# Attention scores from five products of one height: rotary parts of queries and keys stacked to 128 rows per head

## The chip, the cores and the metric

The kernel runs on one core of a Trainium2 chip. The metric is the device time of one execution in microseconds. Engine names in the profile: PE is TensorE (PEld its weight loads), DVE is VectorE, ACT is ScalarE, POOL is GpSimd, SP is SyncE, which issues nearly all DMAs.

## What is computed

Two blocks in a row on 512 tokens of width 1024, all in float32: first a convolution and state-space layer, then two transformer-like layers with feed-forward halves before and after a mixer. The mixer of the second of these layers is latent attention with eight heads; it is the part that matters here:

```python
MLA_HEADS, NOPE_DIM, ROPE_DIM, V_DIM = 8, 128, 64, 128      # QK_DIM = 192
q = (_rmsnorm(c_q, q_a_norm) @ w_q_up).reshape(B, T, 8, 192)
kv = (_rmsnorm(c_kv, kv_a_norm) @ w_kv_up).reshape(B, T, 8, 256)
k = concat([kv[..., :128], broadcast(k_pe)], -1)
q, k = _rmsnorm(q, q_norm), _rmsnorm(k, k_norm)
q = concat([q[..., :128], _rope(q[..., 128:], cos, sin)], -1)
k = concat([k[..., :128], _rope(k[..., 128:], cos, sin)], -1)
s = einsum('bhqd,bkhd->bhqk', q, k) * 192 ** -0.5           # causal mask, softmax
o = einsum('bhqk,bkhd->bqhd', softmax(s), v)
```

A score is a sum over 192 elements per head: 128 without position and 64 rotary ones. The rotary key is the same for all heads but for its norm.

## The kernel before

Activations lie with channels on the 128 partitions and the 512 tokens along the row. Every float32 product is made of three products of a reduced type: each operand is split into a high part (a cast on ACT) and a low part (the rest, a subtraction on DVE), and high x high, high x low and low x high are summed in one bank of PSUM. Weights are streamed by `wload` (L226 to L239): SP loads a tile `raw`, ACT casts it to `wh`, DVE (sometimes POOL) subtracts to `wl`. `mm3` (L241 to L250) issues the three products of L247 to L249.

The program is a row of stages: the first block, a feed-forward half, the mixer `even`, two feed-forward halves, the mixer `odd` (about 2050 to 2350 us on the profile's clock), a last feed-forward half. A list scheduler with priorities sets the order of the instructions on each engine when the kernel is built, so a change anywhere can move instructions elsewhere in the program.

In `odd`, after the projections, heads are worked in four pairs p. `kpair(p)` prepares the keys of a pair: rows of norms are read from a DRAM scratch `nd` and repeated over the partitions (L1781 for the 128-element part, L1785 in two halves of 64 partitions for the rotary part), multiplied by the keys (L1787, on POOL for the tiles in `KP_POOL`, else DVE) and split (L253 and L254) into three tiles high and low: the 128-row part of each of the two heads, and one tile whose lower 64 rows are the rotary key of the first head and whose upper 64 rows that of the second. `qpair(p)` makes the queries in the same layout, two tiles of 128 rows and one shared rotary tile, split at L254 by `P.split(ro, hi, lo)`. `head(h, K, Q)` then works four blocks of 128 queries. Per block b it sums six score products at L1872 over N = 256, 256, 384 and 512 keys, in turns one of 128 rows and one of 64 rows, adds the mask by a product at L1873, and goes on: row maximum (L1875, DVE), scaled negative (L1877, DVE), exponential with sum (L1879, ACT), reciprocal and scaling (L1880 and L1881, DVE), transposes (L1884, PE), split (L1887 on ACT, L1888 on DVE). After four blocks the products with the values follow (L1895 to L1897), all 128 rows high. Two PSUM banks take the scores in turn and two the transposes.

While the heads of pair p run, `kpair(p + 1)` and `qpair(p + 1)` stand between them, in p = 0 also half of the value projection (`vproj(1)`), and from p = 2 on half of the output projection (`outp(0)`), whose products come at L247 to L249 with the name `s`. `TSlots` hands out `OD_S` tiles of 512 columns in turn.

Of the kernel before, what the change touches and what calls it, by code (L numbers as in the profile page):

```python
# [8 lines left out]
F32 = mybir.dt.float32  # L9
# [4 lines left out]
T = 512  # L14
# [142 lines left out]
class Prog:  # L157
    def __init__(self, ctx, tc, ap):
        self.tc, self.nc, self.ap = tc, tc.nc, ap
        nc = self.nc  # L160
        E = ctx.enter_context
        self.const = E(tc.tile_pool(name="const", bufs=1))
        self.res = E(tc.tile_pool(name="res", bufs=1))
        self.wr = E(tc.tile_pool(name="wr", bufs=2))
        self.whp = E(tc.tile_pool(name="whp", bufs=2))
        self.wlp = E(tc.tile_pool(name="wlp", bufs=2))
        psum = E(tc.tile_pool(name="psum", bufs=1, space=PSUM))
        self.banks = [psum.tile([128, T], F32, name=f"bank{i}") for i in range(8)]
        self.rot = {}
        self.use_banks(mm=4, sd=4)  # L170
        self.vec = self.const.tile([128, NVEC], F32, name="vec")
        nc.gpsimd.dma_start(self.vec, ap["vec"])
        self.ones = self.const.tile([128, 128], F32, name="ones")
        nc.vector.memset(self.ones, 1.0)
        self.ident = self.const.tile([128, 128], F32, name="ident")
        nc.gpsimd.affine_select(out=self.ident, in_=self.ones, pattern=[[1, 128]], base=0,
                                channel_multiplier=-1, compare_op=ALU.is_equal, fill=0.0)
        self.eps6 = self.const.tile([128, 1], F32, name="eps6")
        nc.vector.memset(self.eps6, 1e-6)
        self.eps5 = self.const.tile([128, 1], F32, name="eps5")  # L180
        nc.vector.memset(self.eps5, 1e-5)
        self.xa = self.res.tile([128, 8 * T], F32, name="xa")
        self.x = self.cut(self.xa)
        self.new_xhl()
        self.rs = None
        self.ph = None
        self.wlo = nc.vector
# [840 lines left out]
def even(P, nxt):  # L1028
# [8 lines left out]
    with ExitStack() as ctx:  # L1037
# [12 lines left out]
        hw0, ha0, hka, oka = (lambda j, b=b: half[:, 4 * b + j:4 * b + j + 1] for b in range(4))  # L1050
        wn = c("wn", (96, 512))
        wau, nr = wn[0:64], wn[64:96]
        nc.gpsimd.dma_start(wau, ap["lora"])
        gup = c("gup", (96, 512))
        nc.gpsimd.dma_start(gup, ap["g_up"])
        bones = c("bones", (128, 128))
        V.memset(bones, 0.0)
        V.memset(bones[0:64, 0:64], 1.0)
# [538 lines left out]
ATTN_SCALE = 192.0 ** -0.5  # L1597


KP_POOL = [[p, i] for p in (1, 2, 3) for i in range(3)]  # L1600
RO_POOL = True
OD_S = 45
OD_PRIO = {"H": 0, "N": 0, "O": 0, "Z": 10000}
OD_BANKS = dict(mm=2, sd=1, sc=2, pt=2, po=1)

# [1 line left out]
def odd(P, nxt):  # L1607
# [14 lines left out]
    with ExitStack() as ctx:  # L1622
# [13 lines left out]
        ct, st_, kr, kpsq = P.x[0:4]  # L1636
        ang, n1 = S.get(), S.get()
        posi = S.get()
        nc.gpsimd.dma_start(posi.bitcast(mybir.dt.int32), ap["pos"])
        V.tensor_copy(ang, posi.bitcast(mybir.dt.int32))  # L1640
        TS(out=ang, in0=ang, scalar1=P.v("invf", 0), scalar2=None, op0=ALU.mult)
        TS(out=n1, in0=ang, scalar1=1.0 / TWO_PI, scalar2=MAGIC, op0=ALU.mult, op1=ALU.add)
# [131 lines left out]

        def kpair(p):
            kh, kl = [], []
            for i in range(3):
                b = S.get()
                if i < 2:
                    h = 2 * p + i  # L1780
                    nc.sync.dma_start(b, nrow(0, h).to_broadcast([128, T]))  # L1781
                else:
                    for n in range(2):
                        h = 2 * p + n
                        nc.sync.dma_start(b[64 * n:64 * n + 64], nrow(1, h).to_broadcast([64, T]))  # L1785
                src = kgs[2 * p + i] if i < 2 else kr
                (GP if [p, i] in KP_POOL else V).tensor_tensor(out=b, in0=src, in1=b, op=ALU.mult)  # L1787
                hi, lo = S.get(R), S.get(R)
                P.split(b, hi, lo)
                S.put(b)  # L1790
                if i < 2 and p > 1:
                    S.put(src)
                kh.append(hi), kl.append(lo)
            return kh, kl
# [3 lines left out]
        def qpair(p, kind="mm"):  # L1798
# [3 lines left out]
            for i in range(3):  # L1802
# [9 lines left out]
                else:  # L1812
                    qg, ro = S.get(), S.get()
                    A.activation(qg, ps, AF.Copy, scale=P.v("qn", 1))
                    rope(qg, ro)
                    P.split(ro, hi, lo)
                    S.put(qg, ro)
                qh.append(hi), ql.append(lo)
            for n in range(2):
                ns = slice(64 * n, 64 * n + 64)  # L1820
                GP.tensor_tensor(out=sqs[n][ns], in0=sqs[n][ns], in1=sqs[2][ns], op=ALU.add)
# [8 lines left out]
            A.activation(sc, sc, AF.Sqrt)  # L1830
            V.reciprocal(sc, sc)
            TS(out=sc, in0=sc, scalar1=ATTN_SCALE, scalar2=None, op0=ALU.mult)
            return qh, ql, sc

        vh, vl = P.xh, P.xl

# [18 lines left out]

        def head(h, K, Q):
            kh, kl = K
            qh, ql, sc = Q
            hl, i = h % 2, h % 4
            rsl = slice(64 * hl, 64 * hl + 64)  # L1860
            pa, pb_ = pth[hl], ptl[hl]
            for b in range(4):
                n = 128 * (b + 1)
                N = max(256, n)
                bs = slice(128 * b, 128 * b + 128)
                ps = P.bank("sc")
                ops = []
                for qq, kk in ((qh, kh), (qh, kl), (ql, kh)):
                    ops.append((qq[hl][:, bs], kk[hl][:, 0:N]))
                    ops.append((qq[2][rsl, bs], kk[2][rsl, 0:N]))  # L1870
                for m, (x, y) in enumerate(ops):
                    MM(ps[:, 0:N], x, y, start=m == 0, stop=False)  # L1872
                MM(ps[:, n - 128:n], identb, neg, start=False, stop=True)  # L1873
                mx, nb, sm = small("mx"), small("nb"), small("sm")
                V.tensor_reduce(out=mx, in_=ps[:, 0:n], op=ALU.max, axis=mybir.AxisListType.X)  # L1875
# [59 lines left out]
        for p in range(4):  # L1935
# [12 lines left out]
            with tc.issue_after(qlast[0].ins):  # L1948
                head(2 * p, K, Q)
            head(2 * p + 1, K, Q)  # L1950
            for t in K[0] + K[1] + Q[0] + Q[1]:
                S.put(t)
            K, Q = Kn, Qn
        prio("N")
# [42 lines left out]
```

## Time and profile before

| | |
|---|---|
| median of three runs | 2705.6 us (2704.5 to 2705.71) |
| the profiled execution | 2702.08 us |
| its span, first to last instruction | 2700.3 us |
| PE busy | 2595.2 us, 96% of the span |
| DVE busy | 1399.5 us, 52% |
| ACT busy | 954.6 us, 35% |
| POOL busy | 523.8 us, 19% |
| DMA, mean rate | 93 GB/s |

The profile records one execution. A stretch of time is named by microseconds from the start of the span. Products of PE are pipelined: one takes 0.3 to 0.5 us from start to end, but the next can start long before the end. So the cost of a row of products is read from the distance between starts, and a busy share of 100% only says that PE had always something under way. The granted clock is the share of the full 2.4 GHz that the throttle let through.

### The profile page before, as it was taken

Reading aid. Unit: us, or ns where it says so; the run is one execution under the profiler, and the core shown is the slowest. Engines: PE = TensorE matmul, PEld = TensorE weight load, DVE = VectorE, ACT = ScalarE, POOL = GpSimd, SP = SyncE. Lnnn points to the kernel's source line nnn. Section 1 sums busy time; section 2 is a strip of 40 time slices with the busy share of each in tenths; the row PEclk is TensorE's granted clock in tenths of the full one; section 3 lists DMA queues with packets and bytes.
Section 4 is the critical chain, followed back from the end, with each engine's and each line's share of the span. In section 5 each row is a group of like instructions: output and inputs, shape, how many; then the busy total and the mean of one; then the engine's idle time right before and its main releaser. Section 6 shows DMA issues by size and latency. Waiting matters only on the chain.

```text
span 2700.3 us, 32142 instructions
## 1 busy us (share of the span) xinstructions
PE 2595.2 (96%) x12836; PEld 2080.7 (77%) x12836; DVE 1399.5 (52%) x1860; ACT 954.6 (35%) x1361; POOL 523.8 (19%) x382
## 2 busy tenths in 40 slices
PE   6798999989999999999999999999999999999999
PEld 4577887877888867778588888888888666788887
DVE  9955636545434468643654344443444755643442
ACT  4455536243222342222332223322234553432231
POOL 5699502031000055331100000000001311100000
PEclk9898999999999999999999999999999989999999
DMA  3233332322232334123122322322324412122323
GB/s 113 89 96 86 115 107 88 125 79 86 87 108 95 103 120 96 50 67 114 51 94 87 108 94 88 107 95 93 102 91 133 109 40 67 58 99 91 105 89 107
DMA packets 116070, 251.86 MB, mean 93 GB/s; under 512 B 44176, under 2 KB 53008, under 8 KB 115920
## 3 DMA queue, kind: packets, MB, share of 16 engines
q1 hardware_dynamic: 115664, 249.00, 29.4%
q8 instruction: 100, 1.64, 0.3%
q0 software_dynamic: 256, 0.81, 0.1%
q14 instruction: 50, 0.41, 0.0%
HBM read 235.21 MB, written 13.37 MB: 92 GB/s over the span
## 4 chain that ended last, share of the span: by engine, by line
PE 83%; DVE 9%; POOL 2%; issue 2%; ACT 2%; DMA 1%; SPq 0%; DVEq 0%; ACTq 0%; POOLq 0%
PE bank L247 24%; PE bank L249 24%; PE bank L248 23%; PE bank L1872 2%; DVE wl L236 2%; POOL xa L761 1%; PE bank L744 1%; ACT wh L235 1%; PE bank L1228 1%; PE bank L745 1%; POOL acc L264 1%; PE bank L743 1%; PE bank L1424 1%; DMA raw<-in_ffn_dn_dram 0%; DVE xl L270 0%
## 5 line engine op out<-in xcount | busy, mean ns | idle before, releaser
L235 ACT CAST wh<-raw 128x1024 fp32r<-128x1024 f32 (+1 forms) x452 | 437.0, 968 | 1214.2 <-PE bank L248 918.7
L247 PE MATMUL bank<-xh,wh 128*128 128x512 f32 (+1 forms) x2144 | 837.2, 392 | 24.4 <-ACT wh L235 14.8
L248 PE MATMUL bank<-xl,wh 128*128 128x512 f32 (+1 forms) x2144 | 839.9, 392 | 12.3 <-DVE xl L927 6.9
L249 PE MATMUL bank<-xh,wl 128*128 128x512 f32 (+1 forms) x2144 | 841.1, 393 | 10.7 <-DVE wl L236 10.7
L236 DVE TENSOR_TENSOR wl<-raw,wh 128x1024 fp32r<-128x1024 f32 (+1 forms) x418 | 497.1, 1190 | 518.1 <-ACT wh L235 509.3
L247 PEld LDWEIGHTS bank<-xh,wh 128*128 128x128 f32 x2144 | 407.3, 190 | 115.7 <-ACT wh L235 19.5
L249 PEld LDWEIGHTS bank<-xh,wl 128*128 128x128 f32 x2144 | 407.5, 190 | 106.2 <-DVE wl L236 14.6
L248 PEld LDWEIGHTS bank<-xl,wh 128*128 128x128 f32 x2144 | 407.7, 190 | 101.2 <-DVE xl L927 7.7
L264 POOL TENSOR_TENSOR acc<-acc,sq 128x512 f32<-128x512 f32 x54 | 81.5, 1510 | 1349.4 <-ACT sq L263 1348.6
L249 PE MATMUL bank<-mh,wl 128*128 128x512 f32 x704 | 274.6, 390 | 0.4 <-DVE wl L236 0.3
L248 PE MATMUL bank<-ml,wh 128*128 128x512 f32 x704 | 274.2, 390 | 0.0
L247 PE MATMUL bank<-mh,wh 128*128 128x512 f32 x704 | 274.1, 389 | 0.0
L323 DVE TENSOR_TENSOR up<-bank,rs 128x512 f32<-128x512 f32 x88 | 60.8, 691 | 267.1 <-PE bank L249 267.1
L249 PEld LDWEIGHTS bank<-mh,wl 128*128 128x128 f32 x704 | 132.1, 188 | 33.6 <-DVE wl L236 2.0
L319 DVE TENSOR_TENSOR gp<-bank,rs 128x512 f32<-128x512 f32 x88 | 60.8, 691 | 179.6 <-PE bank L249 179.5
L248 PEld LDWEIGHTS bank<-ml,wh 128*128 128x128 f32 x704 | 132.1, 188 | 27.9
L247 PEld LDWEIGHTS bank<-mh,wh 128*128 128x128 f32 x704 | 132.2, 188 | 25.6
L761 POOL TENSOR_TENSOR xa<-xa,cw 128x512 f32<-128x512 f32 x90 | 137.2, 1525 | 26.7 <-ACT cw L760 23.8
L236 POOL TENSOR_TENSOR wl<-raw,wh 128x1024 fp32r<-128x1024 f32 x34 | 82.7, 2433 | 144.2 <-ACT wh L235 140.7
L760 ACT ACTIVATE cw<-cu,hcw 128x512 f32<-128x512 f32 x90 | 64.2, 721 | 52.8 <-POOL xa L761 51.4
L253 ACT CAST mh<-m 128x512 fp32r<-128x512 f32 x88 | 54.9, 625 | 61.6 <-DVE m L325 61.6
L1872 PE MATMUL bank<-s,s 128*128 128x256 f32 (+3 forms) x192 | 72.2, 434 | 0.4 <-ACT s L1879 0.4
(653 smaller groups left out, 2948.1 us busy)
## 6 DMA issues: line engine op xcount, KB each, us to landing
raw<-in_ffn_gu_dram SPq DMA_DIRECT2D x176, 512.0 KB, 3.5
raw<-in_ffn_dn_dram SPq DMA_DIRECT2D x64, 512.0 KB, 3.6
raw<-in_w_in_dram SPq DMA_DIRECT2D x46, 512.0 KB, 3.5
raw<-in_even_in_dram SPq DMA_DIRECT2D x26, 512.0 KB, 3.5
raw<-in_ffn_dn_dram SPq DMA_DIRECT2D x64, 192.0 KB, 3.3
raw<-in_conv_dram SPq DMA_DIRECT2D x20, 512.0 KB, 3.7
xa<-in_xT_dram SPq DMA_DIRECT2D x16, 256.0 KB, 4.2
raw<-in_w_co_dram SPq DMA_DIRECT2D x8, 512.0 KB, 3.3
```

The lines of the kernel that those rows point to most:

```text
L235: nc.scalar.copy(h[:, :m], raw[:, :m])
L236: self.wlo.tensor_tensor(out=l[:, :m], in0=raw[:, :m], in1=h[:, :m].bitcast(F32), op=ALU.subtract)
L247: self.nc.tensor.matmul(ps, h[i][:, s], xh[k], start=a, stop=False)
L248: self.nc.tensor.matmul(ps, h[i][:, s], xl[k], start=False, stop=False)
L249: last = self.nc.tensor.matmul(ps, l[i][:, s], xh[k], start=False, stop=b)
L253: self.nc.scalar.copy(hi, src)
L264: nc.gpsimd.tensor_tensor(out=acc, in0=acc, in1=sq, op=ALU.add)
L319: nc.vector.tensor_tensor(out=gp, in0=pg, in1=rs, op=ALU.mult)
L323: nc.vector.tensor_tensor(out=up, in0=pu, in1=rs, op=ALU.mult)
L760: A.activation(w, cu[:, j:j + T], AF.Copy, scale=hcw[:, 31 * k + j:31 * k + j + 1])
L761: GP.tensor_tensor(out=y, in0=y, in1=w, op=ALU.add)
L1872: MM(ps[:, 0:N], x, y, start=m == 0, stop=False)
```

## The change

Keys get four tiles a pair in place of three: the rotary key is multiplied by one head's norm row over all 128 partitions, so that both halves of a tile hold the same 64 rotary rows (which the projection delivers twice already). Queries get, for each head, one rotary tile `qr` whose one half is the high part and whose other half the low part. A product of `qr` with the key's high tile then sums high x high and low x high at once, and one with the key's low tile adds high x low (and the small low x low). A block has three products of the 128-element part and two of the stacked rotary part, five in all, each 128 rows high.

To make room for four more tiles (`OD_S` 49), the scratch for software DMAs is cut to 1024 bytes, and the four loads that POOL issued go to other queues: the vector of constants to ACT's, the two small weights of `even` and the positions of `odd` to SP's.

```diff
-        nc.gpsimd.dma_start(self.vec, ap["vec"])
+        nc.scalar.dma_start(self.vec, ap["vec"])
...
-        nc.gpsimd.dma_start(wau, ap["lora"])
+        nc.sync.dma_start(wau, ap["lora"])
...
-        nc.gpsimd.dma_start(gup, ap["g_up"])
+        nc.sync.dma_start(gup, ap["g_up"])
...
-KP_POOL = [[p, i] for p in (1, 2, 3) for i in range(3)]
+KP_POOL = [[p, i] for p in (1, 2, 3) for i in range(4)]
...
-OD_S = 45
+OD_S = 49
...
-        nc.gpsimd.dma_start(posi.bitcast(mybir.dt.int32), ap["pos"])
+        nc.sync.dma_start(posi.bitcast(mybir.dt.int32), ap["pos"])
...
-            for i in range(3):
+            for i in range(4):
                 b = S.get()
-                if i < 2:
-                    h = 2 * p + i
-                    nc.sync.dma_start(b, nrow(0, h).to_broadcast([128, T]))
-                else:
-                    for n in range(2):
-                        h = 2 * p + n
-                        nc.sync.dma_start(b[64 * n:64 * n + 64], nrow(1, h).to_broadcast([64, T]))
+                nc.sync.dma_start(b, nrow(i // 2, 2 * p + i % 2).to_broadcast([128, T]))
...
-                    P.split(ro, hi, lo)
+                    for n, b in enumerate((hi, lo)):
+                        a, o = slice(64 * n, 64 * n + 64), slice(64 - 64 * n, 128 - 64 * n)
+                        A.copy(b[a], ro[a])
+                        TT(out=b[o], in0=ro[a], in1=b[a].bitcast(F32), op=ALU.subtract)
...
+            qh, ql, qr = qh[0:2], ql[0:2], [qh[2], ql[2]]
...
-                ops = []
-                for qq, kk in ((qh, kh), (qh, kl), (ql, kh)):
-                    ops.append((qq[hl][:, bs], kk[hl][:, 0:N]))
-                    ops.append((qq[2][rsl, bs], kk[2][rsl, 0:N]))
+                ops = ((qh[hl], kh[hl]), (qh[hl], kl[hl]), (ql[hl], kh[hl]), (qr[hl], kh[2 + hl]), (qr[hl], kl[2 + hl]))
                 for m, (x, y) in enumerate(ops):
-                    MM(ps[:, 0:N], x, y, start=m == 0, stop=False)
+                    MM(ps[:, 0:N], x[:, bs], y[:, 0:N], start=m == 0, stop=False)
...
-    nc = _bacc.Bacc("TRN2", target_bir_lowering=False, num_devices=1)
+    nc = _bacc.Bacc("TRN2", target_bir_lowering=False, num_devices=1, dynamic_dma_scratch_size=1024)
```

On PE, the first block of 384 keys (head 0) reads as follows before. Names are the output, then key and query tile: 14899 and 14900 are the 128-element key, high and low, 14914 and 14915 the shared rotary key, 14941 and 14942 the query, 14971 and 14972 its rotary part.

```order
L1872 MATMUL bank_76<-s_14899,s_14941 128x384
L1872 MATMUL bank_76<-s_14914,s_14971 128x384
L1872 MATMUL bank_76<-s_14900,s_14941 128x384
L1872 MATMUL bank_76<-s_14915,s_14971 128x384
L1872 MATMUL bank_76<-s_14899,s_14942 128x384
L1872 MATMUL bank_76<-s_14914,s_14972 128x384
L1873 LDWEIGHTS identb
L1873 MATMUL bank_76<-neg,identb 128x128
```

Tiles of 128 rows and of 64 rows take turns. With the change, where 14913 and 14914 are the rotary key of this head and 14977 its stacked rotary query:

```order
L1866 MATMUL bank_76<-s_14899,s_14947 128x384
L1866 MATMUL bank_76<-s_14900,s_14947 128x384
L1866 MATMUL bank_76<-s_14899,s_14948 128x384
L1866 MATMUL bank_76<-s_14913,s_14977 128x384
L1866 MATMUL bank_76<-s_14914,s_14977 128x384
L1867 LDWEIGHTS identb
L1867 MATMUL bank_76<-neg,identb 128x128
```

One product is gone, and the two kinds no longer take turns. On SP, the loads ahead of the first heads stand as follows before: `nd` are the rows of norms, `xd` the residual, 14896 and 14903 the tiles of the first pair's two heads, 14910 its rotary tile.

```order
L1765 DMA nd_14659<-s_14643 128x512
L1785 DMA s_15012<-nd_14659 64x512 x2
L1918 DMA xa<-xd_14442 128x512
L1781 DMA s_14998<-nd_14659 128x512
L1781 DMA s_15005<-nd_14659 128x512
L234 DMA raw<-in_q_up_dram 128x1024
L1781 DMA s_14896<-nd_14659 128x512
L1781 DMA s_14903<-nd_14659 128x512
L1785 DMA s_14910<-nd_14659 64x512 x2
L234 DMA raw<-in_q_up_dram 128x128
```

The rotary rows come in pairs of halves, the last of them for the first pair. With the change, where 14910 and 14917 are the rotary tiles of the first pair's two heads and the numbers from 15006 on belong to the second pair:

```order
L1765 DMA nd_14659<-s_14643 128x512
L1912 DMA xa<-xd_14442 128x512
L1779 DMA s_14910<-nd_14659 128x512
L234 DMA raw<-in_q_up_dram 128x1024
L1779 DMA s_15006<-nd_14659 128x512
L1779 DMA s_15013<-nd_14659 128x512
L1779 DMA s_15020<-nd_14659 128x512
L1779 DMA s_14896<-nd_14659 128x512
L1779 DMA s_14903<-nd_14659 128x512
L1779 DMA s_14917<-nd_14659 128x512
L1779 DMA s_15027<-nd_14659 128x512
L234 DMA raw<-in_q_up_dram 128x128
```

The first rotary tile has moved to the front, two halves have become whole tiles, and the small second part of the `q_up` weights stands behind eight loads of norm rows.

## Rows read from the trace of the kernel before

**Rows 1.** Stretches: microseconds; each engine's busy time (instructions), clock, DMA share, GB/s.
```profile
0.00:320.00 320.00, 255.53 (x1280) 207.76 (x1281) 228.63 (x276) 167.02 (x242) 247.13 (x191) 0.89 0.32 96
2135.00:2150.00 15.00, 8.58 (x27) 5.63 (x25) 10.68 (x17) 6.35 (x12) 6.45 (x4) 0.66 0.52 153
2150.00:2260.00 110.00, 108.26 (x436) 73.87 (x435) 66.24 (x153) 56.81 (x115) 24.34 (x18) 0.89 0.16 48
2260.00:2310.00 50.00, 50.00 (x219) 35.07 (x220) 25.71 (x66) 15.40 (x38) 0.00 (x0) 1.00 0.14 42
```
**Rows 2.** Waits of PE, 2150 to 2310: who for whom, us, times, longest.
```profile
PE bank L247 <- DVE s L1811: 1.4, 1, 1.4
```
**Rows 3.** Groups by line, attention stage: busy us, mean ns, then idle before.
```profile
L1872 PE MATMUL bank<-s,s 128*128 128x256 f32 (+3 forms) x192 | 72.2, 434 | 0.4 <-ACT s L1879 0.4
...
L1872 PEld LDWEIGHTS bank<-s,s 64*128 64x128 f32 x96 | 18.4, 192 | 18.9 <-issue 14.1
...
L1875 DVE TENSOR_REDUCE mx<-bank 128x1 f32<-128x128 f32 (+3 forms) x32 | 15.6, 490 | 29.5 <-PE bank L1873 29.3
```
**Rows 4.** Timeline of PE, three score blocks: start, length, then instructions merged.
```profile
2161.30 2.27 PE L1872 MATMUL bank<-s,s 128*128 128x384 f32 x6 [0.39 <-ACT s L1879]
2163.50 0.23 PE L1873 MATMUL bank<-neg,identb 128*128 128x128 bf16 x1
...
2176.53 1.84 PE L1872 MATMUL bank<-s,s 128*128 128x256 f32 x6
2178.30 0.23 PE L1873 MATMUL bank<-neg,identb 128*128 128x128 bf16 x1
...
2303.70 2.53 PE L1872 MATMUL bank<-s,s 128*128 128x512 f32 x6
2306.16 0.23 PE L1873 MATMUL bank<-neg,identb 128*128 128x128 bf16 x1
```
**Rows 5.** Timeline of PE, products with the values of one head.
```profile
2187.92 0.40 PE L1897 MATMUL bank<-pth,xl 128*128 128x512 f32 x1
2188.15 0.34 PE L1895 MATMUL bank<-pth,xh 128*128 128x384 f32 x1
2188.33 0.34 PE L1896 MATMUL bank<-ptl,xh 128*128 128x384 f32 x1
...
2188.68 0.28 PE L1895 MATMUL bank<-pth,xh 128*128 128x256 f32 x1
2188.79 0.28 PE L1896 MATMUL bank<-ptl,xh 128*128 128x256 f32 x1
```
**Rows 6.** Timeline of PE: a score block at the low clock.
```profile
2213.56 2.96 PE L1872 MATMUL bank<-s,s 128*128 128x256 f32 x6
2216.46 0.29 PE L1873 MATMUL bank<-neg,identb 128*128 128x128 bf16 x1
```
**Rows 7.** Two stretches, ahead of the heads and within; columns as in rows 1.
```profile
2130.00:2135.00 5.00, 5.00 (x27) 4.24 (x26) 2.81 (x4) 2.20 (x4) 2.52 (x2) 1.00 1.02 259
...
2215.00:2220.00 5.00, 5.00 (x13) 2.99 (x13) 1.67 (x6) 2.38 (x6) 0.00 (x0) 0.50 0.13 48
```
**Rows 8.** Timeline of DVE: the scaling that ends one block's softmax.
```profile
2308.56 0.49 DVE L1881 TENSOR_SCALAR s<-s,sm 128x512 f32<-128x512 f32 x1
```
**Rows 9.** Groups by line and shape, 2080 to 2350: weight split, key split, key product.
```profile
L236 DVE TENSOR_TENSOR wl<-raw,wh 128x1024 fp32r<-128x1024 f32 x22 | 27.6, 1255 | 6.2 <-ACT wh L235 6.1
...
L254 DVE TENSOR_TENSOR s<-s,s 128x512 fp32r<-128x512 f32 x16 | 12.2, 776 | 4.0 <-PE bank L1884 2.1 <-ACT s L253 1.9
...
L1787 POOL TENSOR_TENSOR s<-xa,s 128x512 f32<-128x512 f32 x5 | 6.4, 1280 | 11.6 <-DMA s<-nd 11.6
```
**Rows 10.** Timelines of POOL and DVE: the positions issued, and first used.
```profile
2083.98 0.60 POOL L1639 DMA_DIRECT2D s<-in_pos_dram  x1 [9.75 <-DVE rs L285]
...
2087.81 0.42 DVE L1640 CAST s<-s 128x512 f32<-128x512 int32 x1
```
**Rows 11.** Timeline of PE: its first product.
```profile
6.24 0.79 PE L247 MATMUL bank<-xh,wh 128*128 128x512 f32 x1 [6.24 <-ACT xh L956]
```

More of the change, by code (lines that the diff above doesn't have):

```diff
@@ L1832, in qpair @@
             TS(out=sc, in0=sc, scalar1=ATTN_SCALE, scalar2=None, op0=ALU.mult)
-            return qh, ql, sc
+            return qh, ql, sc, qr
         vh, vl = P.xh, P.xl
@@ L1857, in head @@
             kh, kl = K
-            qh, ql, sc = Q
+            qh, ql, sc, qr = Q
             hl, i = h % 2, h % 4
-            rsl = slice(64 * hl, 64 * hl + 64)
             pa, pb_ = pth[hl], ptl[hl]
@@ L1950, in odd @@
             head(2 * p + 1, K, Q)
-            for t in K[0] + K[1] + Q[0] + Q[1]:
+            for t in K[0] + K[1] + Q[0] + Q[1] + Q[3]:
                 S.put(t)
```

## The prediction, made before the change was run

> **What bounds the kernel now.** I read the attention stage first, since the change works there, then the engines around it. The table by stretches [rows 1] shows TensorE (PE) busy for 108.3 of the 110 us from 2150 to 2260 and for all 50 us from 2260 to 2310; these 160 us hold the eight heads. The list of waits of PE in them [rows 2] has one entry over a microsecond, 1.4 us. So in this stage time is what PE's own instructions take. Which? The groups by line [rows 3] give the 192 score products of L1872 72.2 us of the 160. That is out of proportion: DVE, which reduces those scores (L1875), sat idle 29.3 us waiting for them.
>
> Why they are dear is seen on the timeline of PE, from the first product of a block to the mask product that follows. Six products of 256 columns take 1.77 us (2176.53 to 2178.30), six of 384 take 2.20, six of 512 take 2.46 [rows 4]: 0.295, 0.367 and 0.41 us each. The products of probabilities and values, same type, all 128 rows high, follow each other in 0.11 us at 256 columns, 0.18 at 384 and 0.23 at 512 [rows 5]. The difference is 0.18 us in all three widths, independent of columns: about one weight load (0.192 us mean for the 64-row ones, which also idle 14.1 us for "issue" ahead of them) [rows 3]. Among equal heights the load runs beneath the product before; between a 128-row and a 64-row product, which alternate here, it stands in line. That is the cost the change touches.
>
> **The change part by part.**
>
> *Score products.* Per block six alternating products become five, all 128 rows high. At the full clock the 32 blocks (16 of 256 columns, 8 of 384, 8 of 512) took 16 x 1.77 + 8 x 2.20 + 8 x 2.46 = 65.6 us. The row of the stage says 72.2; it counts some 2 us in which a block's last product overlaps the mask, and blocks that ran at the low clock: at 2213.56 a 256-column block took 2.90 us [rows 6]. So the products now hold about 70 us. After: five at the spacing of [rows 5], 16 x 5 x 0.115 + 8 x 5 x 0.175 + 8 x 5 x 0.23 = 25.4 us. PE is relieved of **44 us**, of which 40 are certain at the full clock if the spacing is right and 4 are blocks that no longer run at the low one. Lower bound: if the 0.18 us stays with each of the five, 70 x 5/6 leaves a gain of 12.
>
> *Clock.* PE was granted 0.89 in the first stretch [rows 1], down to 0.50, which is 1.2 of 2.4 GHz, around 2215 to 2220 [rows 7], while it was busy throughout, mostly with products of alternating heights. 0.11 x 110 us = 12 us were lost; up to 4 of them are in the products above, so at most 8 more can come back. Denser products speak for that, new gaps (next) against; I take 2.
>
> *New waits.* PE no longer hides the softmax chain. From the mask of a 512-column block to its scaled exponentials the chain ran 2306.16 to 2309.05, 2.9 us, through DVE, ACT and DVE again [rows 4, 8]. In program order the transposes of a block stand some 2 to 5 us of PE work behind its scores, so the chain itself mostly fits. DVE's load is the matter. In the first stretch it has 66.2 us of work [rows 1]. PE's work there shrinks from 110 by the share 137/192 of the 44 us, 31, to 79. Added on DVE: one more split per pair for the fourth key tile and one more for the stacked queries, each at 0.78 us [rows 9] (halving the rows does not halve a duration that goes by columns, as far as rows here tell), over the three pairs prepared in the stretch 4.7 us. So DVE 70.9 beside PE 79, 90%, with in-order queues on both. In the second stretch PE goes from 50 to 37 and DVE stays near 26: no new bound. The nearest row for two such loaded engines is the start of the program, 0 to 320: DVE 71%, POOL 77%, and PE idle 64 of 320 us, 20% [rows 1]. 20% on top of 79 is 16 us; none is the lower end. DVE's own 71 us cannot force more unless it idles too. I take **+10 us**, nearer to the upper end.
>
> *Other added work.* Each pair's fourth key tile needs one product with its norm row: on POOL at 1.28 us for three pairs [rows 9], on DVE for the first. POOL was busy 24.3 of 110 us [rows 1]: hidden. ACT gets two casts more per pair; at 56.8 of 110 it has room. Two row loads of 64 rows become two of 128: 0.25 MB more per pair. The DMA queues were full only at the start, where keys of two pairs and weights come in (259 GB/s, 2130 to 2135) [rows 7]: 0.5 MB is 2 us there. SP's order was changed as well, so that the first head's norm rows stand earlier and the small second part of the next q_up weights later. PE already waits there, with 8.6 busy of 15 us [rows 1]. I take 0, between -1 and +3.
>
> *Loads moved off POOL's queue.* The positions were issued by POOL at 2083.98 and first used at 2087.81 [rows 10]; now they stand on SP between two weight loads, behind nothing that frees later, so 0. The two small even-stage loads stand before a weight load that has slack. The vector load goes to ACT's queue; PE's first product waited 6.24 us for work that needs it [rows 11]: 0 to -1. What these moves do is disturb the schedule of the first 320 us, where most engines' orders change in detail and hardly in structure. The chains there are the same; I take 0 with 6 us either way.
>
> **Sum.** -44 (products) -2 (clock) +10 (waits) +0 = **-36 us** on the profiled execution, 2702.1, whose span is 2700.3; it is 3.5 us, 0.13%, under the median of the runs. From the median 2705.6 that is about 2669.
>
> **The rivals.**
>
> *DVE becomes the bound of the first stretch.* If DVE, at 71 us of work, is kept busy only two thirds of the time, because its in-order queue stands behind weight splits of 1.2 us [rows 9] and operands from POOL, the stretch takes 106, gains 4, and the second stretch gains 10 to 13: 2705.6 - 16 = 2690. For: 90% of load on both engines. Against: in the first stretch DVE waits for PE now, and the second gains in any case. Anything between this and the forecast is possible; half-way is 2680.
>
> *The change doesn't do what it says: the 0.18 us is not a matter of unequal heights.* Then five of six remain and the gain is the 12 us above, less a few for added work: 2696. Against it stand the twelve value products at 0.11 to 0.23 us with equal heights [rows 5]. The Trainium skill has a rule that speaks for this rival: by "TensorE: Matmul & The Clock Gate", Part 3, The mechanism, a weight load overlaps a running product only where the two use different row groups, which five full-height products never do. By that rule the time would be this rival's; the value products, full height and with loads of 0.19 us that hide even under 0.11 us, disagree.
>
> *Slower: the clock stays low.* Place: PE in the first stretch. If the new waits cut its work into short bursts, and it runs at 1.2 GHz throughout, its 79 us (about 71 at the full clock) become 142 where 110 were: +32, less 13 from the second stretch, +19, 2725. The point from which it decides: about 52 of the 71 us of work at the low level. For: a whole 5 us row stands at the low level [rows 7], and where PE idles most, from 2135 to 2150, the mean was 0.66 [rows 1]. Against: the second stretch ran at 1.00 with the most broken order of all. The Trainium skill, same page, Part 1, says that an idle PE falls to half the rate; here it fell while busy as well.
>
> **How the numbers follow.** Forecast, 2655 to 2683: 0.74. Better than 2655, with full clock and no waits (-44 -8 +0 and a few us at the start): 0.06. DVE bound, 2683 to 2695: 0.11. Not what it says: 0.05. Low clock: 0.02; the start of the program losing more than the gain: 0.02. About 0.2%, 5.4 us, is what a measurement of this kernel can tell from no change. The first four cases are faster by more than that, all but 0.02 at their upper edge; the last two are slower. Faster: 0.94; within: 0.02; slower: 0.04. Likeliest 2669. To hold 8 in 10 the range takes the forecast and half of the DVE case: 2654 to 2688.
>
> **What would show it right or wrong.** Right: 160 products in L1866's group with some 26 to 30 us, spaced 0.11 us at 256 columns; the weight loads' "issue" idle gone; DVE's wait for the mask product far below 29 us; the stage from 2150 shorter by 30 to 42 us; new waits of PE for DVE or ACT of 5 to 16 us. Products still spaced 0.29 us refute the first step. Waits over 25 us mean that DVE took over. A mean clock under 0.8 in the stage means the low clock. A changed first 320 us by more than 6 us would make the sum wrong with the mechanism right.

## The result, and the profile after

The changed kernel takes 2683.4 us (median of four, 2681.55 to 2687.08) where the kernel before takes 2705.65 (2704.5 to 2707.52): a ratio of 0.9919, with an interval of 0.9902 to 0.9936. Measured once more, as `after_again` below, it was 0.9917 (0.9897 to 0.9937). So it is 22 us faster, where 36 were forecast; the time lies in the range of 2654 to 2688, near its slow end.

The profiled execution of it took 2687.08 us with a span of 2685.4. Its groups by line in the attention stage (2090 to 2340 us; columns as in [rows 3]) answer to [rows 3]:

```profile
L1866 PE MATMUL bank<-s,s 128*128 128x256 f32 (+2 forms) x160 | 34.6, 351 | 8.0 <-ACT s L1873 8.0
L1866 PEld LDWEIGHTS bank<-s,s 128*128 128x128 f32 x160 | 26.4, 199 | 12.0 <-ACT s L1873 9.8
L1869 DVE TENSOR_REDUCE mx<-bank 128x1 f32<-128x128 f32 (+3 forms) x32 | 15.3, 482 | 1.9 <-PE bank L1867 1.9
L1875 DVE TENSOR_SCALAR s<-s,sm 128x128 f32<-128x128 f32 (+3 forms) x32 | 14.7, 462 | 1.0
```

The score products (L1866) went from 72.2 us to 34.6, the "issue" idle ahead of the weight loads is gone, and VectorE no longer waits for the mask product: 1.9 us in place of 29.3. In exchange the score products wait 8.0 us for ACT, namely for the exponential that still reads the bank they are to fill.

The timeline of PE, four blocks of 256, 384, 512 and again 384 keys (first the five products, then the mask product), answers to [rows 4] and [rows 6]:

```profile
2197.68 0.76 PE L1866 MATMUL bank<-s,s 128*128 128x256 f32 x5
2198.28 0.23 PE L1867 MATMUL bank<-neg,identb 128*128 128x128 bf16 x1
...
2188.12 1.13 PE L1866 MATMUL bank<-s,s 128*128 128x384 f32 x5
2189.09 0.23 PE L1867 MATMUL bank<-neg,identb 128*128 128x128 bf16 x1
...
2290.74 1.32 PE L1866 MATMUL bank<-s,s 128*128 128x512 f32 x5
2291.90 0.23 PE L1867 MATMUL bank<-neg,identb 128*128 128x128 bf16 x1
...
2233.73 1.97 PE L1866 MATMUL bank<-s,s 128*128 128x384 f32 x5 [1.26 <-ACT s L1873]
2235.50 0.33 PE L1867 MATMUL bank<-neg,identb 128*128 128x128 bf16 x1
```

From first product to mask 256 keys take 0.60 us (1.77 before), 384 take 0.97 (2.20), 512 take 1.16 (2.46). The last block took 1.77 for 384 keys, at the low clock, which the stretches show (columns as in [rows 1]):

```profile
0.00:320.00 320.00, 245.25 (x1237) 198.40 (x1238) 223.36 (x272) 165.61 (x241) 246.09 (x190) 0.88 0.31 96
...
2164.00:2245.00 81.00, 71.52 (x367) 58.04 (x366) 61.48 (x138) 52.24 (x107) 28.61 (x20) 0.89 0.24 74
2245.00:2292.00 47.00, 44.59 (x242) 36.28 (x240) 32.63 (x82) 22.07 (x50) 1.29 (x1) 1.00 0.17 51
...
2230.00:2235.00 5.00, 2.65 (x7) 2.06 (x8) 5.00 (x8) 1.93 (x6) 3.88 (x2) 0.61 0.50 138
2235.00:2240.00 5.00, 5.00 (x22) 4.50 (x21) 2.98 (x8) 1.79 (x3) 1.27 (x1) 0.50 0.37 126
```

The clock stood at 0.50 (1.2 of 2.4 GHz) from 2235 to 2240, behind five microseconds in which PE was busy for 2.65. In the first row PE did 10 us less in the first 320 us than in [rows 1]: the first block is late. The waits of PE while the heads run (2164 to 2292; who for whom, us, times, longest), against the single one of [rows 2]:

```profile
PE bank L1866 <- ACT s L1873: 8.0, 7, 2.8
PE bank L1889 <- ACT pth L1881: 2.0, 1, 2.0
PE bank L1708 <- ACT s L1808: 0.9, 1, 0.9
PE bank L247 <- DVE s L1805: 0.6, 1, 0.6
```

**Where the time went.** Two places are common to both traces: the last instructions of the first block (L840) and the reciprocal ahead of the heads (L1762).

```profile
L840 PE MATMUL bank<-sacc,ones x2: 591/592/592, 428.0 to 428.5; 128*128 128x512 f32 x2
...
L1762 DVE RECIPROCAL xa<-s x1: 3345/3345/3345, 2117.5 to 2117.5; 128x512 f32<-128x512 f32 x1
```

These are of before (durations in ns, then first and last start). Of after:

```profile
L840 PE MATMUL bank<-sacc,ones x2: 591/592/592, 435.2 to 435.6; 128*128 128x512 f32 x2
...
L1762 DVE RECIPROCAL xa<-s x1: 3345/3345/3345, 2131.4 to 2131.4; 128x512 f32<-128x512 f32 x1
```

After is 7.2 us late at the end of the first block, 13.9 late ahead of the heads, 14.8 late at the first score product and 14.2 early behind the heads; the rest of the program adds nothing. So the heads gained 29 us and the program ahead of them lost 14. For the heads, from the first score product to the last, one can add up for each product the distance to the next start, less the idle time in it:

| | length | PE's own work | of it score products | PE idle |
|---|---|---|---|---|
| before | 151.5 | 149.8 | 69.3 | 1.7 |
| after | 122.5 | 110.6 | 29.9 | 11.9 |

39.4 us went out of the score products, 10.2 came back as waits; all other work stayed (80.5 and 80.7).

### The profile page after: what moved, and what is told of

Read it like the earlier page. It is cut to its first block, busy times and chain, and to the rows that moved or that the text cites. A ratio compares the mean times of both kernels' runs of the same rounds, so it can differ in the third digit from the quotient of the medians.

```text
span 2685.4 us, 32078 instructions
## 1 busy us (share of the span) xinstructions
PE 2556.2 (95%) x12804; PEld 2067.1 (77%) x12804; DVE 1409.7 (52%) x1869; ACT 958.2 (36%) x1369; POOL 528.9 (20%) x381
## 4 chain that ended last, share of the span: by engine, by line
PE 80%; DVE 9%; POOL 4%; issue 3%; ACT 2%; DMA 1%; SPq 0%; POOLq 0%; DVEq 0%; ACTq 0%
PE bank L247 23%; PE bank L249 23%; PE bank L248 23%; POOL xa L761 2%; DVE wl L236 1%; PE bank L1866 1%; DMA s<-nd 1%; PE bank L744 1%; PE bank L745 1%; PE bank L743 1%; POOL acc L264 1%; ACT wh L235 1%; PE bank L1424 1%; PE bank L1228 0%; POOL tmp L521 0%
## 5 line engine op out<-in xcount | busy, mean ns | idle before, releaser
L249 PE MATMUL bank<-xh,wl 128*128 128x512 f32 (+1 forms) x2144 | 839.7, 392 | 20.4 <-DVE wl L236 20.3
L236 DVE TENSOR_TENSOR wl<-raw,wh 128x1024 fp32r<-128x1024 f32 (+1 forms) x418 | 492.8, 1180 | 516.3 <-ACT wh L235 515.0
L247 PEld LDWEIGHTS bank<-xh,wh 128*128 128x128 f32 x2144 | 406.7, 190 | 121.8 <-ACT wh L235 21.5
L249 PEld LDWEIGHTS bank<-xh,wl 128*128 128x128 f32 x2144 | 407.0, 190 | 115.1 <-DVE wl L236 24.3
L249 PE MATMUL bank<-mh,wl 128*128 128x512 f32 x704 | 274.4, 390 | 0.0
L249 PEld LDWEIGHTS bank<-mh,wl 128*128 128x128 f32 x704 | 132.1, 188 | 32.6 <-DVE wl L236 0.5
L761 POOL TENSOR_TENSOR xa<-xa,cw 128x512 f32<-128x512 f32 x90 | 138.3, 1537 | 29.3 <-ACT cw L760 25.8
L236 POOL TENSOR_TENSOR wl<-raw,wh 128x1024 fp32r<-128x1024 f32 x34 | 82.8, 2435 | 156.5 <-ACT wh L235 93.1
L325 DVE TENSOR_TENSOR m<-up,sg 128x512 f32<-128x512 f32 x88 | 60.8, 692 | 10.9 <-ACT sg L321 2.9
```

Of the source, the lines that this page charges most:

```text
L236: self.wlo.tensor_tensor(out=l[:, :m], in0=raw[:, :m], in1=h[:, :m].bitcast(F32), op=ALU.subtract)
L247: self.nc.tensor.matmul(ps, h[i][:, s], xh[k], start=a, stop=False)
L249: last = self.nc.tensor.matmul(ps, l[i][:, s], xh[k], start=False, stop=b)
L325: nc.vector.tensor_tensor(out=m, in0=up, in1=sg, op=ALU.mult)
L761: GP.tensor_tensor(out=y, in0=y, in1=w, op=ALU.add)
```

## Experiments: is it the change of height that costs?

`grouped` is the kernel before with the six products in another order:

```diff
                 for qq, kk in ((qh, kh), (qh, kl), (ql, kh)):
                     ops.append((qq[hl][:, bs], kk[hl][:, 0:N]))
+                for qq, kk in ((qh, kh), (qh, kl), (ql, kh)):
                     ops.append((qq[2][rsl, bs], kk[2][rsl, 0:N]))
```

> The kernel before with one edit: the six score products of a block in another order, first the three of 128 rows, then the three of 64 rows. Theory: what costs 0.18 us is each change of height between neighbours, six a block when they take turns (the mask product behind included), two when they are grouped. Four changes fewer in 32 blocks are 32 x 4 x 0.18 = 23 us of TensorE's time less; with some waits of 3 to 8 us for VectorE in their place 2685 to 2691 us. Rival 1: every product of such a block pays the 0.18 us for another reason (64-row loads, two-tile layout): no change, 2703 to 2707. Rival 2: only the 64-row loads are exposed, in any order: also near 2705, and the spacing among the three 128-row products stays at 0.29 us for 256 columns, where the theory says 0.12.

Measured: 2675.65 us where before had 2701.6 on that chip, ratio 0.9902 (0.9885 to 0.9918), some 26 us faster, more than was expected. Its timeline of PE, a 256-key and a 512-key block of six products (this kernel is one line longer, so L1873 are the products and L1874 the mask):

```profile
2188.79 1.06 PE L1873 MATMUL bank<-s,s 128*128 128x256 f32 x6
2189.79 0.23 PE L1874 MATMUL bank<-neg,identb 128*128 128x128 bf16 x1
...
2181.95 1.75 PE L1873 MATMUL bank<-s,s 128*128 128x512 f32 x6
2183.63 0.23 PE L1874 MATMUL bank<-neg,identb 128*128 128x128 bf16 x1
```

The same six products take 1.00 us in place of 1.77, and 1.68 in place of 2.46. Both rivals fall. The distances between starts say more; medians in 256-key blocks, us from one product to the next:

| | taking turns (before) | grouped |
|---|---|---|
| 128 rows, next 128 rows | | 0.118 |
| 128 rows, next 64 rows | 0.31 | 0.207 |
| 64 rows behind 128, next 64 rows | | 0.224 |
| 64 rows, next 64 rows | | 0.119 |
| 64 rows, then the mask (128 rows) | 0.31 | 0.209 |

Products of 64 rows among themselves are as cheap as those of 128. A change of height costs about 0.19 us, half of it on the product ahead of it and half on the one behind: 0.09 + 0.10. Where every product stands between two changes it pays both halves, 0.31. The weight loads show the same. Between two products of 128 rows in `grouped` the second one's load starts 0.003 us behind the start of the product ahead (median of 30, 256 columns, full clock); where a product of 64 rows follows one of 128, its load starts 0.206 us behind it (median of 13), and in before, where all products take turns, 0.31. So the step of the prediction that carries the most, the load that stands in line at a change of height, is shown, and by a kernel that has neither the fifth product nor the stacked tiles.

The Trainium skill, "TensorE: Matmul & The Clock Gate", Part 3, The mechanism, says in its list that a load overlaps a running product only where the row groups differ; the paragraph ahead of the list also allows a load into a background weight buffer. Equal row groups at 0.118 us with loads of 0.19 us beneath them, in both heights, and the dearest spacing exactly where the row groups change, say the opposite of the list for these products.

## Experiments: what did the program lose ahead of the heads?

`loads_only` is the kernel before with nothing but the moved loads:

```diff
-        nc.gpsimd.dma_start(self.vec, ap["vec"])
+        nc.scalar.dma_start(self.vec, ap["vec"])
...
-        nc.gpsimd.dma_start(wau, ap["lora"])
+        nc.sync.dma_start(wau, ap["lora"])
...
-        nc.gpsimd.dma_start(gup, ap["g_up"])
+        nc.sync.dma_start(gup, ap["g_up"])
...
-        nc.gpsimd.dma_start(posi.bitcast(mybir.dt.int32), ap["pos"])
+        nc.sync.dma_start(posi.bitcast(mybir.dt.int32), ap["pos"])
...
-num_devices=1)
+num_devices=1, dynamic_dma_scratch_size=1024)
```

> The kernel before with only its four POOL-issued loads moved (vector of constants to ACT's queue, two small even-stage weights and the positions to SP's) and the scratch for software DMAs cut to 1024 bytes; attention as before. Theory A: the changed kernel loses outside attention because of these moves (its trace stands 7.1 us late at the end of the first block and 13.9 us late ahead of the heads, and is not later anywhere behind them). Then this kernel is about 14 us slower than before, 2717 to 2722 us, with some 7 us in the first block and 7 in the even stage. Rival B: the 14 us are the ordinary difference between executions (clock, DMA timing); then it is within 3 us of 2705.6.

`attn_only` is the changed kernel with those four lines as before and a scratch of 8192 bytes, for which the tiles still leave room:

> The changed kernel with its four loads back on POOL and a scratch of 8192 bytes; only the attention is changed against the kernel before. Theory A: the 14 us outside attention come back, the 28 us gained in the heads stay: 2705.6 - 28 = 2678 or a little below, down to 2669 if all 14 us count against the changed kernel's median of 2683.4; first block and even stage within 1 us of before. Rival B: no difference from the changed kernel, 2683.

`vec_back` takes back only the first of the four lines of the changed kernel:

> The changed kernel with only the vector of constants loaded by POOL again; the even-stage weights and the positions stay on SP's queue. Theory A, with one cause per stage: the first block's 7 us come back, the even stage's stay: about 2676 us, between the changed kernel and the one with all four loads back. Rival: both losses hang on the even-stage loads or on the scratch, then 2683.

Measured: `loads_only` 2712.3 us, ratio 1.0049 (1.0032 to 1.0067), slower by 9 to 18 us; `attn_only` 2674.0, 0.9899 (0.9882 to 0.9916); `vec_back` 2679.0, 0.992 (0.9899 to 0.9942). The intervals of the last two overlap that of the changed kernel, so the times alone don't part them. The traces do, at the end of the first block (L840), which `loads_only`, `attn_only` and `vec_back` reach here:

```profile
L840 PE MATMUL bank<-sacc,ones x2: 591/592/592, 433.8 to 434.2; 128*128 128x512 f32 x2
```
```profile
L840 PE MATMUL bank<-sacc,ones x2: 591/592/592, 428.7 to 429.1; 128*128 128x512 f32 x2
```
```profile
L840 PE MATMUL bank<-sacc,ones x2: 591/592/592, 429.2 to 429.7; 128*128 128x512 f32 x2
```

With the vector on ACT's queue it is 5.8 us late (6.0 in `after_again`, 7.2 in after); with the vector on POOL it is 0.7 and 1.2 us behind the 428.0 of before. The cause can be seen on POOL, first before, then after, from 46 us on (start, length, then instructions merged):

```profile
48.45 2.53 POOL L357 TENSOR_TENSOR s5tb<-s5b,s5t 128x512 f32<-128x512 f32 x2 [8.63 <-DVE s5t L416]
50.94 1.33 POOL L357 TENSOR_TENSOR s5bb<-s5bb,s5tb 128x512 f32<-128x512 f32 x1
52.23 1.72 POOL L357 TENSOR_TENSOR s5bbs<-s5bbs,s5tb 128x512 f32<-128x512 f32 x1
54.36 1.55 POOL L761 TENSOR_TENSOR xa<-xa,cw 128x512 f32<-128x512 f32 x1 [0.41 <-ACT cw L760]
58.01 4.98 POOL L521 TENSOR_TENSOR w<-s5c,s5t 128x576 f32<-128x576 f32 x4 [2.10 <-DVE s5t L453]
```
```profile
53.81 2.18 POOL L357 TENSOR_TENSOR s5tb<-s5b,s5t 128x512 f32<-128x512 f32 x2 [14.14 <-DVE s5t L416]
55.95 5.33 POOL L521 TENSOR_TENSOR w<-s5c,s5t 128x576 f32<-128x576 f32 x4
61.25 1.45 POOL L761 TENSOR_TENSOR xa<-xa,cw 128x512 f32<-128x512 f32 x1
```

VectorE's order was planned anew too and feeds POOL 5.4 us later, and POOL then takes four products of L521 ahead of the first of its 90 convolution taps (L761): the taps start 6.9 us late on an engine that is 77% busy [rows 1] and don't catch up. That is the order; it could still be the queue. `vec_sync`, built on `attn_only`, tells the two apart:

```diff
-        nc.gpsimd.dma_start(self.vec, ap["vec"])
+        nc.sync.dma_start(self.vec, ap["vec"])
```

> The changed kernel with the two even-stage weights and the positions back on POOL (scratch 8192 bytes) and the vector of constants on SP's queue instead of ACT's. As in the changed kernel POOL no longer issues the vector; but in the planned order POOL takes the first convolution tap (L761) ahead of the four s5 products of L521 again, as in the kernel before. Theory A (the order on POOL is what costs): first tap at 54 to 56 us in place of 61, the end of the first block (L840) within 1.5 us of before, 2671 to 2676 us. Rival B (taking the vector off POOL's queue, or loading it later, is what costs): the end of the first block 5 to 7 us late, 2678 to 2682 us.

Measured: 2672.4 us, ratio 0.989 (0.9854 to 0.9926). Its first tap and its L840:

```profile
57.01 1.81 POOL L761 TENSOR_TENSOR xa<-xa,cw 128x512 f32<-128x512 f32 x1 [0.41 <-ACT cw L760]
...
L840 PE MATMUL bank<-sacc,ones x2: 591/592/592, 429.6 to 430.1; 128*128 128x512 f32 x2
```

POOL doesn't issue the vector here either, yet the first block ends 1.6 us late and not 6 to 7. The tap started a little later than expected and the end missed its 1.5 us by a tenth; the kernels whose POOL issues the vector spread nearly as far, from 0.9 us early (`keys_dve`) to 1.5 late (`lows_pool`). So rival B, that taking the vector off POOL's queue is itself what costs, is out.

Theory A, that the order on POOL is what costs, fits, but isn't isolated. `vec_sync` has not got the order of before: VectorE, ACT and POOL were planned anew in it as well, and only the first tap stands ahead of the four products again. What the traces show is that the end is late by about as much as the first tap: the tap by 0.6 us in `attn_only`, 0.7 in `vec_back`, 2.7 in `vec_sync` and 6.5 to 6.9 in the three kernels with all loads moved, the end by 0.7, 1.2, 1.6 and 5.8 to 7.2. How much of the late tap is POOL's own order and how much is VectorE feeding it later, these runs don't part.

`after_again` is the changed kernel itself, measured on one chip with the first three kernels of the next section:

> The changed kernel as it is, beside the next three on one chip. Its ratio to the kernel before was 0.9919; the one with the four loads back on POOL had 0.9899 on another chip. If the loads cost what the kernel before loses with them alone (0.49%), this ratio is 0.993 to 0.996 against some 0.990 for the other; if the two edits don't add up, it stays at 0.992.

Measured: 0.9917 (0.9897 to 0.9937), 2685.3 us. It stayed at 0.992, and against the 0.9899 of `attn_only` the times leave open by how much the moved loads slow the whole program; 6 us in the first block are what the traces show.

The other 7 us ahead of the heads are not settled. From L840 to the end of the even stage's L1453 the profiled run of after lost 3.8 us against before. The four kernels with the small weights on SP's queue stand at +3.8, +3.7, +4.0 and 0.0 there; the nine without at -6.9 to +8.3, median -2.5, though eight of the nine have the instruction order of before in that stage. A single trace can't show 4 us in it. From there to the heads the three kernels with all four loads moved lost 2.9 to 3.0 us, the others -0.3 to 2.6; there the loads may have a part, which no run isolates.

## Experiments: what sets the new waits?

The prediction put them down to VectorE, loaded to 90%. Four kernels, all built on `attn_only`, change that load: `keys_dve` has the key products on VectorE, `lows_pool` the low parts of keys on POOL, `scale_act` the scaling of the exponentials on ACT, `lows_scale` the last two together.

```diff
-KP_POOL = [[p, i] for p in (1, 2, 3) for i in range(4)]
+KP_POOL = []
```
```diff
-                P.split(b, hi, lo)
+                A.copy(hi, b)
+                (GP if p else V).tensor_tensor(out=lo, in0=b, in1=hi.bitcast(F32), op=ALU.subtract)
```
```diff
-                TS(out=e[:, 0:n], in0=e[:, 0:n], scalar1=sm, scalar2=None, op0=ALU.mult)
+                A.activation(e[:, 0:n], e[:, 0:n], AF.Copy, scale=sm)
```

> The changed kernel with the four loads back on POOL and all sixteen key products on VectorE (none on POOL): 12 instructions of 0.7 to 0.95 us, 8 to 11 us more for VectorE while the heads run. Theory A, VectorE's load sets the new waits: TensorE's waits in the stage grow by 5 to 10 us, the time by as much, 2680 to 2684 us. Rival B, the waits are the length of each block's own softmax chain: no change, 2672 to 2676; it could even be a little faster, since POOL's products are longer (1.3 to 1.4 us) and stand ahead of the splits.

> The changed kernel with the four loads back on POOL and the low parts of the keys of pairs 1 to 3 (12 subtractions of 0.78 to 0.92 us) made by POOL instead of VectorE: 9 to 11 us less for VectorE while the first five heads run, 15 us more for POOL. Theory A (VectorE's load): of some 11 us of waits in the heads half goes, 2668 to 2670 us. Rival B (chain): 2672 to 2676. Rival C: POOL comes late with the keys, over 2676.

> The changed kernel with the four loads back on POOL and the scaling of the exponentials (32 instructions of 0.35 to 0.6 us, 14.8 us in all on VectorE) made by ACT: VectorE has 15 us less, ACT some 16 to 20 us more, and the chain of a block is as long or 0.1 us longer. Theory A (VectorE's load): waits go from 11 to about 5 us, 2666 to 2670. Rival B (chain): 2673 to 2677, since the chain is not shorter.

> The two kernels with less work on VectorE in one: four loads back on POOL, low parts of the keys of pairs 1 to 3 on POOL, the exponentials scaled by ACT; VectorE has some 25 us less in the stage than in the changed kernel. Their ratios to the kernel before were 0.9865 and 0.9853, that of the kernel with the loads alone 0.9899. If the parts add up: 0.982 to 0.983, 2657 to 2660 us. If the chain of a block sets the waits: no better than the better one, 0.985, 2665 to 2668 us.

Measured, with before and `grouped` beside them; length, score products and idle time are worked out of each trace from the first score product to the last, as in the table above, and the busy times are those of the same stretch:

| kernel | median us | ratio to before (interval) | length | score products | PE idle | DVE busy | POOL busy |
|---|---|---|---|---|---|---|---|
| before | | | 151.5 | 69.3 | 1.7 | 87 | 24 |
| grouped | 2675.65 | 0.9902 (0.9885 to 0.9918) | 124.6 | 42.4 | 4.0 | 88 | 26 |
| attn_only | 2674.0 | 0.9899 (0.9882 to 0.9916) | 120.1 | 28.6 | 12.2 | 90 | 29 |
| keys_dve | 2674.15 | 0.9882 (0.9861 to 0.9904) | 121.8 | 29.0 | 13.5 | 92 | 18 |
| lows_pool | 2671.4 | 0.9865 (0.9843 to 0.9886) | 115.7 | 28.7 | 9.7 | 84 | 39 |
| scale_act | 2667.1 | 0.9853 (0.9833 to 0.9874) | 117.0 | 29.3 | 9.9 | 78 | 29 |
| lows_scale | 2680.5 | 0.99 (0.9866 to 0.9934) | 118.8 | 29.8 | 11.1 | 72 | 39 |

The stretches of `keys_dve`, `scale_act` and `lows_scale`, one row each:

```profile
2154.00:2276.00 122.00, 108.50 (x578) 87.98 (x577) 92.16 (x221) 70.41 (x150) 18.43 (x12) 0.96 0.21 64
```
```profile
2155.00:2272.00 117.00, 107.11 (x575) 87.55 (x574) 78.00 (x182) 83.11 (x178) 28.87 (x20) 0.96 0.22 67
```
```profile
2151.00:2270.00 119.00, 107.91 (x577) 88.16 (x576) 72.49 (x172) 82.97 (x181) 39.44 (x28) 0.94 0.23 66
```

Over these kernels VectorE's load goes from 92 us to 72 of some 120, and PE's idle time from 13.5 to 11.1. It is not VectorE's load that sets most of the waits; the 5 to 10 us expected of the heavier load didn't come, nor did half of the 11 us go with the lighter ones. What relief there is, two to three us of idle time, comes with the first ten us less of load. The test has its limits. In `keys_dve` VectorE's load rose by less than 2 us, since only eight of the twelve products fall between the first and the last score product (5.5 us) and its key splits took 3 us less there, so a much heavier load wasn't tried. And `scale_act` gives ACT more (70 to 83 us) and `lows_pool` gives POOL more (29 to 39), which can take back a part of the relief. `lows_scale` is inconclusive in its time, since its runs spread from 2665.6 to 2685.9, but its stage is no better than those of its parts.

Theory A for the waits fell. The list of waits above names another: PE waits for a score bank that the exponential of two blocks before still reads. `sc3` and `sc3_scale` give the scores a third bank, taken from the transposes; `sc3_scale` scales on ACT as well:

```diff
-OD_BANKS = dict(mm=2, sd=1, sc=2, pt=2, po=1)
+OD_BANKS = dict(mm=2, sd=1, sc=3, pt=1, po=1)
```

> The changed kernel with the four loads back on POOL, three banks for the scores and one for the transposes in place of two and two. Theory A, which the runs with more and with less work on VectorE leave: most of TensorE's new waits are for a score bank that the exponential of two blocks before still reads; with a third bank TensorE gets a block further, these waits (8 us) fall to 2 or less, the time to 2667 to 2670 us, unless the one bank of the transposes gives it back. Rival B: the waits only move to the transposes (same chain, other bank), 2672 to 2676 us. Rival C: the single transposes bank costs more than the third score bank gives, over 2677 us.

> Three score banks and one for the transposes, with the exponentials scaled by ACT, four loads back on POOL. If the bank and VectorE's load are two separate causes: below either alone, 2662 to 2665 us. If the waits only change their place: 2665 to 2670 us, as with the scaling on ACT alone.

Measured: 2705.0 us, ratio 0.9999 (0.998 to 1.0018), and 2709.6 us, 1.0017 (1.0001 to 1.0034): the gain is gone, rival C, at a price far beyond the one expected. The waits of PE in `sc3`, 2165 to 2300:

```profile
PE bank L1866 <- ACT s L1873: 9.5, 6, 3.8
PE bank L1878 <- DVE ptl L1882: 6.8, 7, 1.6
PE bank L247 <- DVE s L1805: 3.7, 2, 2.7
PE bank L1889 <- ACT pth L1881: 2.5, 4, 0.7
```

The transposes (L1878) now wait for VectorE to read their one bank, the scores wait for the exponentials just as before although they have a third bank, and from the first to the last score product PE is idle for 23.7 us. That is not all of the price: the profiled `sc3` is 34.9 us longer than `attn_only`, 13 us in this stretch, 15 behind it, where thirty more transposes and other products of the last heads stand, and 7 ahead of it, where the edit does nothing. So a bank more for the scores buys nothing as long as the steps behind them are held up. The wait belongs to a block's whole chain: maximum, exponential, scaling, transposes, the two reads of their bank. Its pace hangs on the transposes' banks much more than on VectorE's load: with one of them taken away PE idles 11.5 us more than in `attn_only`, while 20 us of VectorE's load move its idle time by less than 4. With all eight banks in use, more of both couldn't be given, so how the 12 us of `attn_only` divide between the chain's length and its two pairs of banks stays open.

One comparison in the table tells most about the change. `grouped` got as much as `attn_only`, 0.9902 against 0.9899. Stacking and the fifth product saved took another 13.8 us off the score products (42.4 to 28.6), and 8.2 of them came back as idle time of PE.

`scale_act` is faster than both kernels of this case: 0.9853 to before, where the changed kernel had 0.9917 on the same chip.

## The prediction, step by step

- **What bounds the kernel, and the 0.18 us at a change of height: right.** `grouped` shows it: 0.19 us, in two halves.
- **Score products, -44 us: mis-sized, -39.4.** The 70 us of before were 69.3. The spacing forecast for after is right: the medians are 0.119, 0.178 and 0.234 us at 256, 384 and 512 columns, which make 26.0 for all 160, beside 25.4. Of the other 3.9 us, 2.1 are thirteen products that got less than the full clock, as in the block at 2233.73; the step assumed that no score block would run there any more. The remaining 1.9 are first products of blocks at the full clock: behind a mask product, a transpose or a wait they take 0.20 to 0.22 us at 256 columns, behind a weight product (L249) 0.12. The step priced the first product of a block like the rest.
- **Clock, -2 us: near nothing.** All other work of PE between first and last score product took 80.5 us before and 80.7 after.
- **New waits, +10 us: the size right, 10.2, the reason wrong.** They were sized by a share of idle time at the start of the program and blamed on VectorE at 90%; it was busy for 61.48 of 81 us, 76%, in the first stretch of after. The share was also read wrongly: 64 us idle beside 256 of work are 25% on top, so the upper end was 20 us and not 16, and that 10 came out is partly luck. VectorE's load moves the waits by little; by the lists of waits they are the blocks' own chains, which PE covers no more. The text held that this chain "mostly fits" under PE's other work. That sentence failed.
- **Start of the heads, 0 (-1 to +3): right.** Late by 13.9 us ahead and by 14.8 at the first score product.
- **Stage shorter by 30 to 42: just missed.** 29.0 us, by the products' term.
- **Loads moved, and the first 320 us, 0 with 6 either way: the step that failed.** The load's queue and its wait were looked at, and on them it was right: the first product came 0.2 us later than in [rows 11]. But the plan of the whole first block was made anew, and it put POOL's taps 6.9 us back. The loss was 7.2 us in the profiled run, and 5.8 and 6.0 in two others with that order. The prediction named this case, over 6 us there with the mechanism right, and this is what happened.
- **The rivals.** "Not what it says" is refuted, by rows and by `grouped`. The low clock didn't take over: 0.93 on average from 2169 to 2292. The time of 2683 sits at the lower edge of the "DVE is the bound" case, but not for its reason. That it lies in the range is in part luck: the range reached to 2688 for that case, and what used the room was the first block.

The terms as measured, -39.4 + 0.2 + 10.2 + 0.9 for the heads and +6 to 7 for the first block, make -21 to -22 us, which is the difference of the medians. The profiled pair, spans of 2700.3 and 2685.4, differs by 14.9 us only; the even stage and what follows up to the heads are 6.7 us longer in it. They are 6.6 us longer in `after_again` too, so a part of that may be the change's, and that the sum without it meets the medians may be chance.

## What to carry to other kernels

Keep products of one height side by side: in this kernel one added line that only reorders the products gave as much as a new layout with more tiles, more splits and more DMA. Once the products of a chain get cheap, look at which bank or step the next block waits for before taking more work off them. And where a program is planned as a whole, a moved load is not a small edit: compare the order on every loaded engine, above all where the first long series starts on the busiest one.

## Not expected of the hardware

- Products of 64 rows follow each other as fast as those of 128 (0.119 us at 256 columns), and the price of a change of height falls half on the product ahead of it.
- VectorE's subtractions of two operands in SBUF slow down beside POOL. The weight splits of L236 with 1024 columns take 1.22 us with no POOL instruction under way (median of 292, trace of before) and 2.05 us with one under way for over 80% of the time (35 of them). The key splits (L254) averaged 994 ns in after and 776 in `keys_dve`, where POOL has no key products:

```profile
L254 DVE TENSOR_TENSOR s<-s,s 128x512 fp32r<-128x512 f32 x16 | 15.7, 994 | 3.3 <-ACT s L253 3.2
```
```profile
L254 DVE TENSOR_TENSOR s<-s,s 128x512 fp32r<-128x512 f32 x16 | 12.2, 776 | 0.0
```

  In before, with nine key products on POOL, they average 776 too: what counts is whether the two meet. Seven of the sixteen splits took over 1 us in after and two in before and in `keys_dve`, each with POOL at work for about half of it or more. That is a part of why the products moved to VectorE cost it so little in `keys_dve`. The Trainium skill, "SBUF — State Buffer", Who interferes with whom, has a VectorE instruction with two SBUF inputs contend with reads of GpSimd; these rows agree.
- Halving the rows of a subtraction doesn't halve it: the two 64-row halves of a stacked query take 687 ns each on VectorE in `attn_only`, as much as one split of 128 rows with POOL idle (about 680).
